# Gate projection on contiguous rows, and convolution taps kept in DRAM, in a streaming-encoder layer

## The chip, the cores and the metric

The kernel runs on all 8 cores of one Trainium2 chip. The time is the device time of the slowest core, in microseconds (us). The unchanged kernel takes about 1606 us.

Most executions of one kernel agree within 0.3%. In some executions here the cores of one die, or of both, show a lower TensorE clock and the time is some 3 to 15% longer.

## The reference

One layer: a half-step FFN, then a mixing stage with chunked attention and a depthwise convolution side by side, then another half-step FFN.

```python
D_MODEL = 1024; BATCH = 4; SEQ = 4096
D_ATTN = 512; N_HEADS = 8; D_CONV = 512; CONV_WIDTH = 31; D_FF = 2816

x = x + 0.5 * swiglu(rmsnorm(x, g1), ...)               # FFN 1
z = rmsnorm(x, mix_norm) @ w_in                         # q | k | v | a | b, 512 each
attn_out = chunk_band_attention(q, k, v, rel_bias)      # 64-frame chunks, 576-key band
g  = a * sigmoid(b)                                     # the gate product (GLU)
dw = causal depthwise conv of g, width 31, + bias
conv_out = silu(layernorm(dw))
x = x + concat(attn_out, conv_out) @ w_out
x = x + 0.5 * swiglu(rmsnorm(x, g2), ...)               # FFN 2
y = rmsnorm(x, final_norm)
```

## The kernel before

Each core computes 2048 rows, in two groups (0 and 1) of 768 and 1280 rows; activations stand transposed, with channels on the 128 partitions and rows along the free dimension. Each group passes through FFN 1, the mixing stage and FFN 2.

All instructions are placed by a list scheduler that runs when the program is built. It has a cost model: a duration for every operation and a landing time for every DMA. Each engine then executes its instructions **in that fixed order** (in the changed kernel DVE stands still for 21.02 us before a copy while an attention product waits behind it), so a wrong duration in the model does not only misjudge a time, it can also put instructions at places where they block others.

```python
def op(self, e, fn, dur, reads=(), writes=(), inc=True):
    start = max(self.t[e], ...)            # when the model thinks its inputs are there
    self.t[e] = start + dur                # dur: the model's cost figure
    E.items.append(("op", fn, inc))        # its fixed place in the engine's stream

def dma(self, e, fn, semname, nbytes, ..., late=2.0):
    beg = max(self.t[e], self.dma_free)
    self.dma_free = beg + nbytes / 300e3
    fin = max(self.dma_free, ...) + late   # when the model thinks it lands

def act(out, in_, func, n, ...):   P.op("act", ..., 0.19 + n / 1400.0, ...)
def dve(fn, n, ..., rate=960.0):   P.op("dve", fn, 0.07 + n / rate, ...)
def pool(fn, n, reads, writes):    P.op("pool", fn, 0.1 + n / 700.0, reads, writes)
```

Weights pass through a ring buffer in one fixed order, called pieces. POOL's DMA queue loads a piece as soon as the pieces that stood in its place are released. The convolution is 16 x 9 matmuls per group with "spread taps": matrices of 128 x 2304 bf16 per piece, mostly zeros. They are made in the ring, by a multiplication on POOL or DVE, each time they are needed:

```python
for c in range(4): addp((gi, "ab", c), wab_d[c], 2048)         # gate weights
for j in range(4): addp((gi, "K", j), wk_d[j], 1024)
for i in range(8):
    if i == VPOS: addp((gi, "V"), wv_d, 4096)
    addp((gi, "cv", i), i, 2304)                               # taps: made, not loaded
for j in range(4): addp((gi, "Q", j), wq_d[j], 1024)
for i in range(2): addp((gi, "wo%d" % i), wout_d[i], 4096)     # w_out, 1 MB each
for i in range(6): addp((gi, fi, "gu", i), wgu_d[fi][i], 4096) # next FFN, 1 MB each

def issue_weights():
    while ws["next"] < len(pieces):
        p = pieces[ws["next"]]
        # ... return while a piece that overlaps p is not released ...
        if isinstance(p.src, int):
            (pool, dve)[p.src % 2](lambda h: h.tensor_tensor(out=o_, in0=i0, in1=i1, op=ALU.mult),
                                   p.n, ("cmp", "cb"), (("w", p.id),))
            continue
        P.dma("pool", lambda h: h.dma_start(out=dst, in_=src), ...)
```

The gate projection wants its result in *phase order* (all rows 0, 4, 8, ..., then 1, 5, 9, ...), because the convolution works on four phases. It gets that order by streaming the input `hT` with every fourth column:

```python
def glu(g):
    ...
    for ab, b in ((1, bB), (0, bA)):
        for kc in range(8):
            rhs = hT[:, kc, c0:c0 + n].rearrange("p (u s) -> p s u", s=4)
            mm(b, 0, wv[:, ab, kc, :], rhs, n, kc == 0, kc == 7, ...)
    act(tt, bb, AF.Sigmoid, ...)
    gd = gTs[gi][:, c, :, ua:ua + n // 4]
    dve(lambda h: h.tensor_tensor(out=gd, in0=a4, in1=t4, op=ALU.mult), ...)   # a4, t4: views in phases
    # after channels 1 and 3: DMA to DRAM (gscr) and back as gp, with phases on the partitions
```

The convolution's output takes a similar way. After its layer norm it is stored to DRAM (`cscr`), read back in another layout, and copied by DVE into `cvt`, the operand of w_out. I call the load the **way back** and the copies the **cvt copies**. They run beside the attention, whose last step, the **attention product**, is on DVE too; PE may not start the next head pair's product with V before it, because it empties the PSUM banks.

```python
def conv_ln(g):
    ...
    for pc in range(2):
        for p4 in range(4):
            P.dma("sp", ... dma_start(out=cr_d..., in_=co...))                 # cscr <- dreg
    for j in range(4):
        P.dma("sp", ... dma_start(out=c2s..., in_=cr_d...), ..., late=4.0)     # dreg <- cscr, the way back
    for s in g.main:
        for c in range(4):
            yield lambda: max(P.est("dve", (("c2", gi, c),)) - 0.2, P.t["dve"] - 1.0)
            dve(lambda h: h.tensor_copy(out=o_, in_=i_), 4 * un, ...)          # cvt copy

def fin1(u):                                                                   # in attention
    ...
    for e in range(2):
        dve(lambda h: h.tensor_tensor(out=o_, in0=i0, in1=i1, op=ALU.mult), n, # attention product
            (("ps", 4 + e), ("rs", ri)), (("q", gi, j, s),))
```

The softmax here doesn't subtract the row's maximum and nothing guards it: scores larger than these inputs give would overflow.

Of the kernel before, what the change touches and what calls it, by code (L numbers as in the profile page):

```python
# [8 lines left out]
BF16 = mybir.dt.bfloat16  # L9
AF = mybir.ActivationFunctionType  # L10
ALU = mybir.AluOpType
# [34 lines left out]
B_I32 = 2560  # L46
# [198 lines left out]
def build_nc(debug=None):  # L245
# [13 lines left out]
    wv_d = din("wv", [128, 4096])  # L259
    gs_d = [nc.dram_tensor("gscr%d" % g.gi, [32, 16, 4, g.U + g.hist // 4], BF16).ap() for g in G]  # L260
# [7 lines left out]
    with ExitStack() as es:  # L268
# [43 lines left out]
        Pb = carve(O_P, 4096, BF16).rearrange("p (i e t) -> p i e t", i=2, e=2)  # L312
        tmpF = carve(O_RS, 4096, F32).rearrange("p (i t) -> p i t", i=2)
# [9 lines left out]
        stage = carve(O_ACC, CB_N * 4, F32)  # L323
        kM = at_f[:, 0:4 * TMAX].rearrange("p (j t) -> p j t", j=4)
# [44 lines left out]
        for i in range(2):  # L369
            P.reg(("P", i), "d", O_P + 2048 * i, O_P + 2048 * (i + 1))  # L370
            P.reg(("tmpF", i), "d", O_RS + 2048 * i, O_RS + 2048 * (i + 1))
            P.reg(("rs", i), "d", O_RS + 2048 * i, O_RS + 2048 * (i + 1))
# [4 lines left out]
        P.reg("gph", "d", O_GP, O_GP + 16 * 2 * GW)  # L377
        P.reg("stage", "d", O_ACC, O_ACC + CB_N * 4)
# [45 lines left out]
        def pool(fn, n, reads, writes):  # L424
            P.op("pool", fn, 0.1 + n / 700.0, reads, writes)
# [9 lines left out]
        class Piece:  # L435
            def __init__(self, src, ncols):
                self.src, self.n = src, ncols
                self.off = None
                self.issued = False
                self.released = False  # L440
# [4 lines left out]
        def addp(name, src, n):  # L445
            p = Piece(src, n)
            p.id = len(pieces)
            pieces.append(p)
            wp[name] = p
        for gi in range(2):  # L450
            for fi in range(2):
                if fi == 1:
# [4 lines left out]
                    for i in range(8):  # L457
                        if i == VPOS:
                            addp((gi, "V"), wv_d, 4096)
                        addp((gi, "cv", i), i, 2304)  # L460
# [21 lines left out]
        def issue_weights():  # L482
            while ws["next"] < len(pieces):
# [6 lines left out]
                if isinstance(p.src, int):  # L490
                    o_ = ring[:, p.off:p.off + p.n].rearrange("p (a c) -> p a c", c=32)
                    i0 = cmp_t[:, 72 * p.src:72 * (p.src + 1)].unsqueeze(2).broadcast_to([128, 72, 32])
                    i1 = cb[:, B_I32:B_I32 + 32].unsqueeze(1).broadcast_to([128, 72, 32])
                    (pool, dve)[p.src % 2](
                        lambda h, o_=o_, i0=i0, i1=i1: h.tensor_tensor(out=o_, in0=i0, in1=i1, op=ALU.mult), p.n,  # L495
                        ("cmp", "cb"), (("w", p.id),))
                    continue
                k = 2 if p.id == 0 else 1
                w = p.n // k
                for i in range(k):  # L500
# [3 lines left out]
                          "w0" if p.id == 0 else "w%d" % (1 + p.id % 16), 512 * w, reads=(), writes=(("w", p.id),),  # L504
                          issue=1.0, total=2 if p.id == 0 else None)
# [294 lines left out]
        def glu(g):  # L800
# [9 lines left out]
            if True:  # L810
                for c, (s, c0, n) in todo:
# [19 lines left out]
                    for ab, b in ((1, bB), (0, bA)):  # L831
                        for kc in range(8):
                            rhs = hT[:, kc, c0:c0 + n].rearrange("p (u s) -> p s u", s=4)
# [6 lines left out]
                    ua = (c0 - g.H + g.hist) // 4  # L840
                    gd = gTs[gi][:, c, :, ua:ua + n // 4]
                    a4 = ab_.rearrange("p (s u) -> p s u", s=4)
                    t4 = tt.rearrange("p (s u) -> p s u", s=4)
                    dve(lambda h, gd=gd, a4=a4, t4=t4: h.tensor_tensor(out=gd, in0=a4, in1=t4, op=ALU.mult), n,
                        (("ps", bA), ("rs", ti)), (("g", gi, c),))
# [355 lines left out]

        def setup_tables():
# [5 lines left out]
            for hh in range(8):  # L1208
# [14 lines left out]
                yield lambda: P.t["dve"] - 1.0  # L1223
            hv = stage[:, CB_HV:CB_HV + 64]
# [25 lines left out]
        S.add(1, setup_tables())  # L1250
        loads += [(G[1], s) for s in G[1].ids]
# [167 lines left out]
```

## Time and profile before

| Before | value |
|---|---|
| median of 6 runs | 1605.91 us (1605.15 to 1709.28; two slow runs, 1684.16 and 1709.28) |
| spans of the cores in the profiled run | 1594.9 to 1605.5 us |
| mean granted TensorE clock of the cores | 0.979 to 0.985 |

The page's first part gives each engine's busy time, share of the span and number of instructions; its fourth part follows the chain of work that ended last and gives the share of each engine in it.

```profile
PE 1503.6 (94%) x8535; PEld 815.3 (51%) x8670; DVE 545.4 (34%) x867; ACT 457.0 (28%) x762; POOL 296.8 (18%) x334
...
PE 82%; issue 4%; DVE 4%; POOL 4%; ACT 3%; DMA 2%; SPq 0%; POOLq 0%; DVEq 0%; ACTq 0%
```

TensorE (PE) bounds the kernel: it is busy for 94% of the span and is 82% of the chain.

The next lines are from the timeline of PE in the second mixing stage. The columns are start, length in us, engine, line of the program, operation, output <- inputs, sizes, and the number of instructions in the row. Line 414 is the helper that issues every matmul, so rows are told apart by their operands: `psA<-hT,ring` is here the gate, `ps<-hT,ring` the K projection.

```profile
1023.91 7.39 PE L414 MATMUL psA<-hT,ring 128*128 128x512 bf16 x16
...
1031.36 1.67 PE L414 MATMUL ps<-hT,ring 128*128 128x512 bf16 x7
```

A gate matmul of 512 columns takes about 7.39 / 16 = 0.46 us, a K matmul on contiguous columns of the same `hT` 1.67 / 7 = 0.24 us with the pipeline's tail, 0.216 us in longer rows. The stride of four bf16 doubles the cost.

The taps, in the groups of costliest instructions (busy us, mean ns of one, idle time before them and its releasers):

```profile
L495 POOL TENSOR_TENSOR ring<-cmp_sb,cb_sb 128x2304 bf16<-128x2304 bf16 x8 | 33.3, 4159 | 108.3 <-PE psA L414 93.4 <-PE ps L414 14.9
L495 DVE TENSOR_TENSOR ring<-cmp_sb,cb_sb 128x2304 bf16<-128x2304 bf16 x8 | 31.8, 3978 | 1.6 <-issue 1.6
```

What PE waited for, in us in total, number of times, longest. L1132 is the attention product, L969 the convolution's bias, L495 a tap multiplication:

```profile
PE ps L414 <- DVE dreg L1132: 10.6, 11, 1.7
PE ps L414 <- DVE dreg L969: 8.7, 3, 5.9
...
PE ps L414 <- POOL ring L495: 2.1, 1, 2.1
```

From the chain that ended last (start, length in us, what):

```profile
472.78 26.47 DMA cscr<-dreg
501.37 3.78 DMA dreg<-cscr
```

A store to `cscr` took 26.47 us, while four weight loads of 1 MB were in flight; the way back itself took 3.78 us.

### The profile page before, as it was taken

The page shows a single profiled execution, that of the slowest core. Times are in us where ns is not written, and L with a number is a line of the kernel's source. Part 1 is how long each engine was busy: PE and PEld are TensorE (multiplying, and loading weights), DVE is VectorE, ACT ScalarE, POOL GpSimd, SP SyncE. Part 2 cuts the span into 40 slices and gives each one's busy share as a digit, 9 for nine tenths or more (in the row PEclk, how much of TensorE's full clock was granted, in tenths as well). Part 3 has the DMA queues.
Part 4 walks back from the last instruction along what each step waited for, and adds up shares of the span by engine and source line. Part 5 has one row for each costly group of instructions (what it writes and reads, how often), then busy time and mean ns, then how long its engine had stood idle before and what let it go on. Part 6 is the DMA issues. An engine that isn't in the chain of part 4 may idle for free.

```text
span 1605.5 us, 23614 instructions; the slowest of 8 cores (1594.9 to 1605.5 us)
## 1 busy us (share of the span) xinstructions
PE 1503.6 (94%) x8535; PEld 815.3 (51%) x8670; DVE 545.4 (34%) x867; ACT 457.0 (28%) x762; POOL 296.8 (18%) x334
## 2 busy tenths in 40 slices
PE   8899999989878899978999999999878999999996
PEld 5455555543534566644555554434434455555553
DVE  1432221263432522227322222624633442222226
ACT  2321011232176410145110112311386741101123
POOL 2300000251610300063000002503600320000023
PEclk9999999999999999999999999999979999999998
DMA  8342423350434466522943323203242044242313
GB/s 183 92 73 40 73 50 62 60 106 11 77 62 91 100 125 118 102 43 53 227 91 57 73 50 56 40 17 60 43 85 61 1 80 72 40 73 53 60 33 132
DMA packets 29985, 117.41 MB, mean 73 GB/s; under 512 B 7088, under 2 KB 12336, under 8 KB 22064
## 3 DMA queue, kind: packets, MB, share of 16 engines
q0 software_dynamic: 15552, 84.04, 29.9%
q1 hardware_dynamic: 14320, 31.85, 6.7%
q8 instruction: 72, 1.18, 0.3%
q14 instruction: 41, 0.34, 0.1%
HBM read 187.30 MB, written 12.62 MB: 125 GB/s over the span
## 4 chain that ended last, share of the span: by engine, by line
PE 82%; issue 4%; DVE 4%; POOL 4%; ACT 3%; DMA 2%; SPq 0%; POOLq 0%; DVEq 0%; ACTq 0%
PE psA L414 52%; PE ps L414 28%; POOL ssum L568 3%; PE ps L405 2%; DVE hT L605 2%; DMA cscr<-dreg 2%; ACT dreg L418 2%; ACT L418 1%; DVE dreg L1132 1%; DVE dreg L605 0%; DVE xres L747 0%; POOL ssb L573 0%; ACT sq L418 0%; POOL dreg L983 0%; POOL ring L495 0%
## 5 line engine op out<-in xcount | busy, mean ns | idle before, releaser
L414 PE MATMUL psA<-hT,ring 128*128 128x512 bf16 (+2 forms) x4185 | 813.1, 355 | 15.7 <-DVE hT L605 11.7
L414 PEld LDWEIGHTS psA<-hT,ring 128*128 128x128 bf16 x4256 | 418.9, 100 | 404.5 <-issue 91.1
L418 ACT ACTIVATE dreg<-psA 128x512 f32<-128x512 f32 (+3 forms) x350 | 217.2, 625 | 826.1 <-PE psA L414 818.4
L414 PE MATMUL ps<-at,ring 128*128 128x512 bf16 (+1 forms) x1909 | 344.9, 341 | 2.8 <-ACT rstd L418 1.1
L717 DVE TENSOR_TENSOR at<-psA,dreg 128x512 bf16<-128x512 f32 (+1 forms) x242 | 143.9, 595 | 520.4 <-PE psA L414 499.5
L414 PEld LDWEIGHTS ps<-at,ring 128*128 128x128 bf16 x1936 | 189.4, 98 | 156.1 <-issue 3.6
L568 POOL TENSOR_TENSOR ssum<-ssum,sq 128x512 f32<-128x512 f32 (+1 forms) x132 | 137.4, 1041 | 245.1 <-ACT sq L418 233.5
L747 DVE SCALAR_TENSOR_TENSOR xres<-ps,xres 128x512 f32<-128x512 f32 (+1 forms) x176 | 103.3, 592 | 218.7 <-PE ps L414 214.5
L418 ACT ACTIVATE sq<-xres 128x512 bf16<-128x512 f32 (+1 forms) x140 | 76.5, 554 | 130.1 <-DVE xres L747 73.1
L503 POOL DMA_DIRECT2D ring<-wgu x45 | 24.3, 540 | 467.7 <-PE psA L414 231.0
L414 PE MATMUL ps<-dreg,ring 128*128 128x512 bf16 (+3 forms) x599 | 91.7, 310 | 11.9 <-DVE dreg L969 8.7
L605 DVE SCALAR_TENSOR_TENSOR hT<-xres,cs_sb,rstd 128x512 bf16<-128x512 f32 (+1 forms) x120 | 88.8, 793 | 38.7 <-ACT rstd L418 38.7
L414 PEld LDWEIGHTS ps<-dreg,ring 128*128 128x128 bf16 x608 | 57.5, 99 | 40.9 <-issue 13.6
L414 PE MATMUL ps<-hT,ring 128*128 128x512 bf16 (+1 forms) x342 | 65.7, 347 | 0.6 <-issue 0.2
L405 PE MATMUL ps<-cb_sb 128*128 128x256 bf16 x460 | 57.1, 285 | 9.3 <-POOL ssb L573 4.3
L418 ACT ACT_TABLE_LOAD x39 | 50.0, 1283 | 40.5 <-PE psA L414 15.3
L495 POOL TENSOR_TENSOR ring<-cmp_sb,cb_sb 128x2304 bf16<-128x2304 bf16 x8 | 33.3, 4159 | 108.3 <-PE psA L414 93.4
L405 PEld LDWEIGHTS ps<-cb_sb 128*128 128x128 bf16 x460 | 46.9, 102 | 12.3 <-issue 4.5
L414 PE MATMUL ps<-dreg,at 128*128 128x256 bf16 (+3 forms) x222 | 39.3, 284 | 13.7 <-ACT dreg L418 8.3
L414 PEld LDWEIGHTS ps<-hT,ring 128*128 128x128 bf16 x352 | 34.9, 100 | 30.5 <-issue 4.8
L1132 DVE TENSOR_TENSOR dreg<-ps,dreg 64x512 bf16<-64x512 f32 (+1 forms) x40 | 23.3, 582 | 71.5 <-ACT dreg L418 70.8
L503 POOL DMA_DIRECT2D ring<-wdA x16 | 8.4, 528 | 207.3 <-PE psA L414 207.3
(68 smaller groups left out, 610.9 us busy)
## 6 DMA issues: line engine op xcount, KB each, us to landing
ring<-wgu POOLq DMA_DIRECT2D x43, 1024.0 KB, 9.7
ring<-wdA POOLq DMA_DIRECT2D x16, 768.0 KB, 7.7
ring<-wdB POOLq DMA_DIRECT2D x16, 640.0 KB, 7.3
yout<-dreg SPq DMA_DIRECT2D x3, 2048.0 KB, 6.7
ring<-wab POOLq DMA_DIRECT2D x8, 512.0 KB, 8.1
xres<-xin SPq DMA_DIRECT2D x2, 2048.0 KB, 20.2
ring<-wout POOLq DMA_DIRECT2D x4, 1024.0 KB, 13.2
xres<-xin SPq DMA_DIRECT2D x6, 512.0 KB, 8.4
```

Source lines behind the costliest of these rows:

```text
L405: P.op("pe", lambda h: h.matmul(o, lhsT=onesS, rhs=cb[:, B_ONES:B_ONES + 256], start=True, stop=True, skip_group_check=True), 0.11, ("cb1" ...
L414: P.op("pe", lambda h: h.matmul(o, lhsT=lhsT, rhs=rhs, start=start, stop=stop, skip_group_check=True), max(n / 2370.0, 0.06) if dur is Non ...
L418: P.op("act", lambda h: h.activation(out=out, in_=in_, func=func, **kw), 0.19 + n / 1400.0, reads, writes)
L495: lambda h, o_=o_, i0=i0, i1=i1: h.tensor_tensor(out=o_, in0=i0, in1=i1, op=ALU.mult), p.n,
L503: P.dma("pool", lambda h, dst=dst, src=src: h.dma_start(out=dst, in_=src), "w0" if p.id == 0 else "w%d" % (1 + p.id % 16), 512 * w, reads= ...
L568: pool(lambda h: h.tensor_tensor(out=ss, in0=ss, in1=sqt, op=ALU.add), n, (("ssum", r), ("sq", i)), (("ssum", r),))
L605: dve(lambda h, dst=dst, xin=xin, gcol=gcol: h.scalar_tensor_tensor(out=dst, in0=xin, scalar=gcol, in1=rt, op0=ALU.mult, op1=ALU.mult), n, ...
L717: dve(lambda h, at=at, ub=ub, tt=tt: h.tensor_tensor(out=at, in0=ub, in1=tt, op=ALU.mult), n, (("ps", bU), ("tmpF", ti)), (("AT", gi, fl, ...
L747: dve(lambda h, xo=xo, bk=bk: h.scalar_tensor_tensor(out=xo, in0=bk, scalar=0.5, in1=xo, op0=ALU.mult, op1=ALU.add), n, (("ps", b), xk), ( ...
L1132: dve(lambda h, o_=o_, i0=i0, i1=i1: h.tensor_tensor(out=o_, in0=i0, in1=i1, op=ALU.mult), n, (("ps", 4 + e), ("rs", ri)), (("q", gi, j, s),))
```

## The change

It has two intended parts, and it also corrects one figure of the cost model.

1. **Gate part.** The gate matmuls stream contiguous columns. The product goes to a small tile `gn`; one more copy per tile, by ACT or DVE, puts it into phase order.
2. **Tap part.** The spread taps are made once, by POOL near the start, written to DRAM as bf16, and loaded through the ring like weights, 0.59 MB a piece.
3. **Figure.** The cost of a POOL operation in the model goes from 0.1 + n/700 to 0.25 + n/650 us.

```diff
+    cw_d = nc.dram_tensor("cwscr", [8, 128, 2304], BF16).ap()
+        gn = carve(O_P, 2048, BF16).rearrange("p (i t) -> p i t", i=2)
+        cwb = carve(O_GP, 9216, BF16).rearrange("p (i c) -> p i c", i=2)
...
-            P.op("pool", fn, 0.1 + n / 700.0, reads, writes)
+            P.op("pool", fn, 0.25 + n / 650.0, reads, writes)
...
-                        addp((gi, "cv", i), i, 2304)
+                        addp((gi, "cv", i), cw_d[i], 2304, (("cw", i),))      # reads: its store has landed
...
-                if isinstance(p.src, int):
-                    ...  (the multiplication on POOL or DVE)
...
-                            rhs = hT[:, kc, c0:c0 + n].rearrange("p (u s) -> p s u", s=4)
+                            rhs = hT[:, kc, c0:c0 + n]
...
+                    dve(lambda h, ...: h.tensor_tensor(out=gnt, in0=ab_, in1=tt, op=ALU.mult), n, ...)
                     gd = gTs[gi][:, c, :, ua:ua + n // 4]
-                    dve(lambda h, ...: h.tensor_tensor(out=gd, in0=a4, in1=t4, op=ALU.mult), n, ...)
+                    g4 = gnt.rearrange("p (u s) -> p s u", s=4)
+                    if P.t["act"] < P.t["dve"]:
+                        act(gd, g4, AF.Copy, n, ...)
+                    else:
+                        dve(lambda h, ...: h.tensor_copy(out=gd, in_=g4), n, ...)
...
+        def setup_conv():
+            yield lambda: P.est("pool", ("cmp", "cb"), ()) if ("tables",) in F else INF
+            for i in range(8):
+                ...
+                P.op("pool", lambda h, ...: h.tensor_tensor(out=o_, in0=i0, in1=i1, op=ALU.mult), 4.1,
+                     ("cmp", "cb"), (("cwb", i % 2),))
+                P.dma("sp", lambda h, ...: h.dma_start(out=cw_d[i], in_=w_), "cw%d" % i, 256 * 2304, ...)
...
+            F.add(("tables",))         # in setup_tables, just before its last step, 16 small casts on DVE
...
+        S.add(1.5, setup_conv())
```

More of the change, by code (lines that the diff above doesn't have):

```diff
@@ L369, in build_nc @@
         for i in range(2):
+            P.reg(("gn", i), "d", O_P + 1024 * i, O_P + 1024 * (i + 1))
             P.reg(("P", i), "d", O_P + 2048 * i, O_P + 2048 * (i + 1))
@@ L377, in build_nc @@
         P.reg("gph", "d", O_GP, O_GP + 16 * 2 * GW)
+        for i in range(2):
+            P.reg(("cwb", i), "d", O_GP + 4608 * i, O_GP + 4608 * (i + 1))
         P.reg("stage", "d", O_ACC, O_ACC + CB_N * 4)
@@ L435, in build_nc, with __init__ @@
         class Piece:
-            def __init__(self, src, ncols):
-                self.src, self.n = src, ncols
+            def __init__(self, src, ncols, reads):
+                self.src, self.n, self.reads = src, ncols, reads
                 self.off = None
@@ L443, in build_nc, with addp @@
         wp = {}
-        def addp(name, src, n):
-            p = Piece(src, n)
+        def addp(name, src, n, reads=()):
+            p = Piece(src, n, reads)
             p.id = len(pieces)
@@ L489, in issue_weights @@
                 p.issued = True
-                if isinstance(p.src, int):
-                    o_ = ring[:, p.off:p.off + p.n].rearrange("p (a c) -> p a c", c=32)
-                    i0 = cmp_t[:, 72 * p.src:72 * (p.src + 1)].unsqueeze(2).broadcast_to([128, 72, 32])
-                    i1 = cb[:, B_I32:B_I32 + 32].unsqueeze(1).broadcast_to([128, 72, 32])
-                    (pool, dve)[p.src % 2](
-                        lambda h, o_=o_, i0=i0, i1=i1: h.tensor_tensor(out=o_, in0=i0, in1=i1, op=ALU.mult), p.n,
-                        ("cmp", "cb"), (("w", p.id),))
-                    continue
                 k = 2 if p.id == 0 else 1
@@ L503, in issue_weights @@
                     P.dma("pool", lambda h, dst=dst, src=src: h.dma_start(out=dst, in_=src),
-                          "w0" if p.id == 0 else "w%d" % (1 + p.id % 16), 512 * w, reads=(), writes=(("w", p.id),),
-                          issue=1.0, total=2 if p.id == 0 else None)
+                          "w0" if p.id == 0 else "w%d" % (1 + p.id % 16), (256 if p.reads else 512) * w,
+                          reads=p.reads, writes=(("w", p.id),), issue=1.0, total=2 if p.id == 0 else None)
         def wsl(p, view):
@@ L840, in glu @@
                     ua = (c0 - g.H + g.hist) // 4
+                    gi_ = nxt("gn", 2)
+                    gnt = gn[:, gi_, 0:n]
+                    dve(lambda h, gnt=gnt, ab_=ab_, tt=tt: h.tensor_tensor(out=gnt, in0=ab_, in1=tt, op=ALU.mult), n,
+                        (("ps", bA), ("rs", ti)), (("gn", gi_),))
                     gd = gTs[gi][:, c, :, ua:ua + n // 4]
-                    a4 = ab_.rearrange("p (s u) -> p s u", s=4)
-                    t4 = tt.rearrange("p (s u) -> p s u", s=4)
-                    dve(lambda h, gd=gd, a4=a4, t4=t4: h.tensor_tensor(out=gd, in0=a4, in1=t4, op=ALU.mult), n,
-                        (("ps", bA), ("rs", ti)), (("g", gi, c),))
+                    g4 = gnt.rearrange("p (u s) -> p s u", s=4)
+                    if P.t["act"] < P.t["dve"]:
+                        act(gd, g4, AF.Copy, n, (("gn", gi_),), (("g", gi, c),))
+                    else:
+                        dve(lambda h, gd=gd, g4=g4: h.tensor_copy(out=gd, in_=g4), n, (("gn", gi_),), (("g", gi, c),))
                     left[c] -= 1
@@ L1200, in wout @@
             F.add(("wout", gi))
+        def setup_conv():
+            yield lambda: P.est("pool", ("cmp", "cb"), ()) if ("tables",) in F else INF
+            i1 = cb[:, B_I32:B_I32 + 32].unsqueeze(1).broadcast_to([128, 72, 32])
+            for i in range(8):
+                yield lambda: P.est("pool", (), (("cwb", i % 2),))
+                w_ = cwb[:, i % 2, :]
+                o_ = w_.rearrange("p (a c) -> p a c", c=32)
+                i0 = cmp_t[:, 72 * i:72 * (i + 1)].unsqueeze(2).broadcast_to([128, 72, 32])
+                P.op("pool", lambda h, o_=o_, i0=i0: h.tensor_tensor(out=o_, in0=i0, in1=i1, op=ALU.mult), 4.1,
+                     ("cmp", "cb"), (("cwb", i % 2),))
+                P.dma("sp", lambda h, w_=w_, i=i: h.dma_start(out=cw_d[i], in_=w_), "cw%d" % i, 256 * 2304,
+                      reads=(("cwb", i % 2),), writes=(("cw", i),), issue=0.6)
         def setup_tables():
```

## The prediction

> **What bounds it now.** TensorE. The page's busy table gives PE 1503.6 of 1605.5 us (94%), the chain that ended last is 82% PE, and the granted clock is 0.98. DVE (34%), ACT (28%) and POOL (18%) matter only where PE waits for them.
>
> **What the change removes.**
> 1. The gate projection (GLU) streams hT with every fourth column, to leave the result in phase order. In the chain such a matmul of 512 columns takes 452 ns (14.46 us for 32; 7.23 us for 16); the K projection, on contiguous columns of the same hT, takes 216 ns, and the FFN 217 ns. [...]this trace says a stride of four doubles the cost. GLU streams 4 x 16 x (768 + 1280) = 131,072 columns in the two groups (plus 32-column pieces). At 0.883 against 0.421 ns a column that is 60.5 us of PE: 22.7 in the first group (window 347–403 us), 37.8 in the second (1024–1100 us). PE is saturated in both windows, so nearly all of it is on the path.
> 2. Sixteen tap multiplications (L495: 8 on POOL at 4.16 us, 8 on DVE at 2.6 to 9.6 us) in the mixing stage. Off PE, but PE waits behind them: at 351 us a POOL one stretches two DVE norm ops to 4.99 us (PE idle 3.1); in the first convolution gaps of 0.56 + 2.27 + 2.10 us; in the second 5.89 us, behind a 9.6 us DVE tap. [...]Sum on the path: about 14 us.
>
> **What it adds.**
> - 20 products plus 20 strided copies: about 0.77 us on DVE (like the 128x512 copies of L1044) or 0.6 on ACT. A unit takes PE 3.45 us, so they hide, except the last before each transfer to phase order: 2 x 0.8 us.
> - Eight POOL tap multiplications, once (33 us). The tables are ready about 96 us, when POOL has finished the starting norms (last at 72 us) and is idle until about 300 us but for weight issues. Cost 0 to 2 us.
> - 16 loads of 0.59 MB as bf16 by POOL's queue. The comparable loads land in 5 to 10 us, in order with V (issued after the last K matmul). cv5 to cv7 may come a few us late; V matmuls fill. About 2 us.
> - New waits: GLU's 3.45 us units catch up with the norm of the last 256-column block, so K matmuls (17 us in all per group) are used sooner, and less remains to cover the 11 to 13 us from the last gate product to gp landing. I allow 4 us a group, 8 in all.
>
> **Sum.** 1606 - 60.5 - 14 + 1.6 + 1 + 2 + 8 = 1544; 80% range 1530 to 1558. Chances: faster 0.97, same 0.025, slower 0.005.
>
> **What would show each step.** Timeline: GLU matmuls of 512 at about 216 ns, GLU of 16 in 3.45 us; PE busy near 1445 us with the same number of matmuls. Groups: L495 gone from the mixing stages, eight POOL multiplications near 100 to 150 us, all L605 norm ops near 1 us. Waits: PE behind DVE L969 and POOL ring falls from 11 to about 2 us; new PE waits before the first convolution matmul, at most 5 us a group. FFN stages unchanged within 1 us each.
>
> **What would make it wrong.** A lower granted clock once GLU runs dense; tap loads queueing behind V so that the convolution stalls with nothing to fill; the scheduler, whose cost model changed, ordering attention worse; POOL taps at the start delaying norms or weight loads.

No term of the sum goes with them; it came to 1606 - 60.5 - 14 + 1.6 + 1 + 2 + 8 = 1544 us, and the 14 us are the waits read from the trace (3.1 + 0.56 + 2.27 + 2.10 + 5.89).

## More of the kernel before

One more view matters later: DVE's timeline in the first attention (L1132 attention product, L1044 cvt copy; in brackets the idle time before the row, and what ended it).

```profile
476.39 1.41 DVE L1132 TENSOR_TENSOR dreg<-ps,dreg 64x512 bf16<-64x512 f32 x2 [4.52 <-ACT dreg L418]
...
495.98 1.41 DVE L1132 TENSOR_TENSOR dreg<-ps,dreg 64x512 bf16<-64x512 f32 x2 [8.07 <-ACT dreg L418]
...
505.24 1.31 DVE L1044 COPY dreg<-dreg 128x512 bf16<-128x512 bf16 x2 [7.85 <-DMA dreg<-cscr]
```

The cvt copies wait 7.85 us for the way back. In this order it harms little: three attention products (one row each, for a pair of heads) stand before the copies, and PE never waits over 1.7 us for one.

## The result, and the profile after

| | before | after |
|---|---|---|
| median, us | 1606.43 (20 runs, the later ones included; at least 3 of them slow) | 1584.07 (10 runs, 2 of them slow) |
| range, us | 1605.15 to 1709.28 | 1580.11 to 1730.44 |
| ratio of fast runs, 95% interval | | 0.9858 (0.9849 to 0.9868) |
| spans of the cores, profiled run | 1594.9 to 1605.5 us | 1566.6 to 1583.1 us |
| granted clock of the cores | 0.979 to 0.985 | 0.971 to 0.978 |

A ratio here and below is the mean time of one kernel's fast runs over that of the other's in the same rounds, so it is not quite the ratio of the medians quoted. The change saves 1.4%, within the 2% that counts as the same. The prediction, 1544 us with a range of 1530 to 1558, was wrong by 40 us.

The same parts of the page after:

```profile
PE 1473.2 (93%) x8826; PEld 826.3 (52%) x8826; DVE 518.8 (33%) x860; ACT 464.3 (29%) x783; POOL 297.4 (19%) x350
...
PE 78%; DMA 5%; DVE 5%; issue 4%; ACT 3%; POOL 3%; SPq 1%; DVEq 0%; POOLq 0%; ACTq 0%
```

PE's share of the chain fell from 82% to 78%, and DMA's rose from 2% to 5%: the chain now passes through transfers. The span fell by 22 us, but PE's work fell by more than it seems. Its busy time counts filler matmuls, which the scheduler places into PE's waits and whose result nobody uses: their group rose from 460 matmuls in 57.1 us to 616 in 75.0 us. The rest of PE's work fell by 48 us.

The gate itself did what it should. PE's timeline, after:

```profile
1024.23 3.62 PE L420 MATMUL psA<-hT,ring 128*128 128x512 bf16 x16
...
1029.52 10.52 PE L420 MATMUL psA<-hT,ring 128*128 128x512 bf16 x48
```

That is 10.52 / 48 = 0.219 us a matmul, 3.62 us for sixteen instead of 7.39. The copies into phase order all went to ACT; in the groups the ones of 512 columns read:

```profile
L424 ACT ACTIVATE dreg<-dreg 128x512 bf16<-128x512 bf16 x12 | 8.0, 669 | 19.5 <-DVE dreg L841 19.5
```

What PE waits for has changed (slowest core, core 1; L1135 is the attention product, L765 a copy of a Q tile out of PSUM, L715 an FFN product):

```profile
PE ps L420 <- DVE dreg L1135: 22.8, 10, 19.1
PE ps L420 <- DVE dreg L765: 16.2, 1, 16.2
...
PE psA L420 <- DVE at L715: 5.4, 1, 5.4
```

Three single waits, of 19.1, 16.2 and 5.4 us, come to 40.7 us, about the size of what is missing; the stages below and the experiments have to say whether that is more than a coincidence. To place them, I read the first matmul of every stage from the timelines of all eight cores. The table gives the median length of each stage over the cores, in us (the some 30 us before the first FFN matmul and 11 after the last matmul are in no row).

| stage | before | after | difference |
|---|---|---|---|
| start and FFN 1, group 0 | 314.8 | 318.9 | +4.1 |
| gate and K, group 0 | 68.6 | 48.5 | -20.1 |
| convolution, group 0 | 39.8 | 38.3 | -1.5 |
| attention and w_out, group 0 | 90.8 | 105.7 | +14.9 |
| FFN 2, group 0, and start of group 1 | 201.7 | 204.4 | +2.7 |
| FFN 1, group 1 | 274.1 | 274.0 | -0.1 |
| gate and K, group 1 | 90.8 | 57.6 | -33.2 |
| convolution, group 1 | 43.2 | 40.5 | -2.7 |
| attention and w_out, group 1 | 134.2 | 138.8 | +4.6 |
| FFN 2, group 1 | 301.7 | 303.2 | +1.5 |

In the ninth row the cores differ: 132.5 to 135.5 us before, but 135.5 to 148.0 after. On the slowest cores that stage lost some 13 us or more, and it is the slowest core that sets the time. So the gate stages give 53.3 us and the convolutions 4.2; some 15 + 14 us go in the two attentions, 4 at the start, 4 elsewhere.

What happens in the first attention shows in DVE's timeline (core 1; L1135 attention product, L1047 cvt copies):

```profile
456.98 1.41 DVE L1135 TENSOR_TENSOR dreg<-ps,dreg 64x512 bf16<-64x512 f32 x2 [1.81 <-ACT dreg L424]
...
483.18 2.72 DVE L1047 COPY dreg<-dreg 128x512 bf16<-128x512 bf16 x5 [21.02 <-DMA dreg<-cscr]
485.70 1.43 DVE L1135 TENSOR_TENSOR dreg<-ps,dreg 64x512 bf16<-64x512 f32 x2
```

and in PE's:

```profile
486.54 1.31 PE L420 MATMUL ps<-dreg,vh 128*128 128x512 bf16 x2 [19.13 <-DVE dreg L1135]
```

The copies now stand after the *first* attention product rather than the third. DVE comes to them at 462 us and does nothing else until the way back lands at 483 us; the second attention product stands behind them, and PE stands behind that. DMA issues of the same stretch, with KB each and the median us from issue to landing, say why the landing is late:

```profile
ring<-wout POOLq DMA_DIRECT2D x2, 1024.0 KB, 14.1
ring<-wgu POOLq DMA_DIRECT2D x2, 1024.0 KB, 20.5
...
dreg<-cscr SPq DMA_DIRECT2D x4, 192.0 KB, 23.7
```

Four weight loads of 1 MB are issued between 452.0 and 462.2 us, around the four small ones of the way back (452.5 us). These take 23.7 us, where the model adds 4 us to the time of the bytes (`late=4.0`).

The 16.2 us wait in group 1 is of the same kind, on cores 1 and 2: PE waits there for a copy of a Q tile that stands behind the cvt copies in DVE's order. The trace also shows why the cores differ. On core 0 the last store to `cscr` is issued at 1145.97 us, before the first w_out load at 1146.66, and every store lands within 2.8 us; on core 1 the last two are issued at 1149.48 and 1150.01 us, after that load at 1149.11, and land some 17 us later, so that the way back starts at 1168.27 us instead of 1149.43; core 2 is the same. (Core 5 shows the late stores too, but with w_out at 1141.58 us, and ends between.) So less than a microsecond between two queues goes with some 10 us of this stage.

A gap also costs clock. The stretches of core 1 (us of the window, its length, busy time of PE, PEld, DVE, ACT, POOL, then the granted clock, the share of the DMA engines and GB/s):

```profile
467.00:486.00 19.00, 0.41 (x4) 0.12 (x2) 2.82 (x6) 0.91 (x1) 0.00 (x0) 0.59 0.79 153
486.00:490.00 4.00, 3.32 (x16) 1.03 (x16) 2.12 (x5) 0.97 (x1) 0.00 (x0) 0.50 0.00 0
490.00:494.00 4.00, 3.93 (x36) 2.12 (x32) 0.00 (x0) 2.51 (x4) 0.00 (x0) 0.91 0.00 0
```

After the gap PE runs at half clock for some 4 us: 0.50, against 1.00 before it (455 to 467 us); in e4_hold below, which takes the wait away, the clock is 1.00 in every stretch from 455 to 498 us (core 1). So the lower mean clock of the kernel after, 0.971 to 0.978, looks like a consequence of the waits rather than a cause of the loss; the mean clock of e4_hold, 0.980 to 0.986, agrees.

### The profile page after: what moved, and what is told of

Read it like the earlier page. It is cut to its first block, busy times and chain, and to the rows that moved or that the text cites. A ratio compares the mean times of both kernels' runs of the same rounds, so it can differ in the third digit from the quotient of the medians.

```text
span 1583.1 us, 24095 instructions; the slowest of 8 cores (1566.6 to 1583.1 us)
## 1 busy us (share of the span) xinstructions
PE 1473.2 (93%) x8826; PEld 826.3 (52%) x8826; DVE 518.8 (33%) x860; ACT 464.3 (29%) x783; POOL 297.4 (19%) x350
## 4 chain that ended last, share of the span: by engine, by line
PE 78%; DMA 5%; DVE 5%; issue 4%; ACT 3%; POOL 3%; SPq 1%; DVEq 0%; POOLq 0%; ACTq 0%
PE psA L420 49%; PE ps L420 27%; DMA dreg<-cscr 3%; PE ps L411 2%; DVE hT L603 2%; POOL ssum L566 2%; ACT dreg L424 2%; DMA cscr<-dreg 1%; DMA dreg<-gscr 1%; ACT L424 1%; DMA gscr<-dreg 1%; DVE xres L745 1%; DVE vh L1245 1%; DVE dreg L603 0%; POOL ssb L571 0%
## 5 line engine op out<-in xcount | busy, mean ns | idle before, releaser
L420 PE MATMUL psA<-hT,ring 128*128 128x512 bf16 (+2 forms) x4256 | 763.5, 341 | 19.5 <-DVE hT L603 12.9
L420 PEld LDWEIGHTS psA<-hT,ring 128*128 128x128 bf16 x4256 | 414.2, 99 | 364.4 <-issue 42.7
L715 DVE TENSOR_TENSOR at<-psA,dreg 128x512 bf16<-128x512 f32 (+1 forms) x242 | 143.8, 595 | 520.5 <-PE psA L420 496.8
L420 PE MATMUL ps<-hT,ring 128*128 128x512 bf16 (+1 forms) x352 | 66.1, 343 | 16.2 <-DVE dreg L765 16.2
L411 PE MATMUL ps<-cb_sb 128*128 128x256 bf16 x616 | 75.0, 282 | 4.3 <-DVE cb_sb L1253 4.3
L411 PEld LDWEIGHTS ps<-cb_sb 128*128 128x128 bf16 x616 | 62.3, 101 | 14.3 <-issue 4.3
L1135 DVE TENSOR_TENSOR dreg<-ps,dreg 64x512 bf16<-64x512 f32 (+1 forms) x40 | 23.3, 583 | 73.6 <-ACT dreg L424 73.0
L420 PE MATMUL ps<-dreg,vh 128*128 128x128 bf16 (+2 forms) x64 | 15.0, 313 | 29.3 <-DVE dreg L1135 21.3
```

The costliest lines, as they stand in the source:

```text
L411: P.op("pe", lambda h: h.matmul(o, lhsT=onesS, rhs=cb[:, B_ONES:B_ONES + 256], start=True, stop=True, skip_group_check=True), 0.11, ("cb1" ...
L420: P.op("pe", lambda h: h.matmul(o, lhsT=lhsT, rhs=rhs, start=start, stop=stop, skip_group_check=True), max(n / 2370.0, 0.06) if dur is Non ...
L715: dve(lambda h, at=at, ub=ub, tt=tt: h.tensor_tensor(out=at, in0=ub, in1=tt, op=ALU.mult), n, (("ps", bU), ("tmpF", ti)), (("AT", gi, fl, ...
L1135: dve(lambda h, o_=o_, i0=i0, i1=i1: h.tensor_tensor(out=o_, in0=i0, in1=i1, op=ALU.mult), n, (("ps", 4 + e), ("rs", ri)), (("q", gi, j, s),))
```

## The experiments

**Theory A (collision and order).** Both parts save what they should, but the new fixed order puts the cvt copies in front of the attention products while the way back is under way beside four weight loads. A smaller loss is at the start, where the taps on POOL hold up the last casts of the tables on DVE.

**Rival R (the tap part itself).** Sixteen more loads of 0.59 MB disturb everything else, so the tap part costs more than it saves wherever it is used, and the gate part alone would reach about 1550 us.

**Rival, the figure.** The corrected POOL figure alone reorders the program for the worse.

Experiments e1, e2, e4 and e5 were timed on one chip, e3, e8_all, e8v and e9 on a second, e0, e10 and e11 on a third, each beside the kernel before (fast median 1606 to 1608 us).

### e1_glu: the gate part alone

The kernel before with the gate part and the new POOL figure; taps as before.

```diff
-                            rhs = hT[:, kc, c0:c0 + n].rearrange("p (u s) -> p s u", s=4)
+                            rhs = hT[:, kc, c0:c0 + n]
+                    (gn, the product and the copy as in the change; 0.25 + n / 650.0)
```

> Only the gate part of the change (contiguous rows, product, copy; the POOL cost figure of the changed kernel kept); the taps are made in place in the mixing stages as before. Theory A (the gate saves what was forecast, and the gain is then given back in attention, where VectorE waits in order for the way back from channel order, plus small losses at the start and at the tap loads): stage from first GLU to first convolution matmul about 49 and 58 to 60 us as in the changed kernel, first FFN back to 274 us, attention of the first group still lengthened by 5 to 15 us; time 1565 to 1585 us. Rival R (the taps' way through DRAM eats the gain): time near 1550 us and no lengthened attention.

Measured: 1564.33 us (1562.1 to 1564.4), ratio 0.9732 (0.9715 to 0.9748), correct. Gate stages 51.2 and 60.0 us instead of 68.6 and 90.8; first attention 94.8.

The gate part alone is worth 42 us, and 20 us *more* than the whole change. The time lies just under the range of theory A and well over what R wanted, so both missed, A by less than a microsecond. A's mechanism did not show here either: the first attention is 4.0 us longer than before, but that comes with the POOL figure alone (94.8 us in e0_figure below), and the copies stand behind five attention products. What follows for certain is only that the tap part, as it stands in this order, costs some 20 us.

### e2_taps: the tap part alone

The changed kernel with the strided gate put back.

```diff
-                            rhs = hT[:, kc, c0:c0 + n]
+                            rhs = hT[:, kc, c0:c0 + n].rearrange("p (u s) -> p s u", s=4)
+                    (the product straight into phase order, as before)
```

> Only the tap part (made once on POOL, written to DRAM, 16 loads); the gate matmuls stride as before. Theory A: 1596 to 1612 us: the first FFN 5 to 8 us longer, each convolution waits about 5 us for its last taps, the old tap waits gone. Rival R: 1630 us or more, with the loss in the mixing stages.

Measured: fast runs 1635.38 to 1642.12 us (one slow run, 1805), ratio 1.0198 (1.0173 to 1.0222), correct. First attention 105.8 us, second 135.4 to 146.8 over the cores, start 321.3.

Theory A's forecast for this run missed: I had thought the order went wrong only with both parts together. R had the size. But the loss stands in the same places as in the full change: a PE gap of 19.1 us behind the attention product, 15.6 behind a Q copy, 5.3 at the start. So the tap part brings the bad order. Whether the extra loads also cost something where they stand needs the next runs.

### e4_hold: w_out loads held until the way back has landed

The transfers no longer collide. The two w_out pieces, and with them all that follow in the ring, are issued only after the way back. The order of instructions on PE, ACT, DVE and SP stays exactly as in the changed kernel, and POOL's too.

```diff
-                        addp((gi, "wo%d" % i), wout_d[i], 4096)
+                        addp((gi, "wo%d" % i), wout_d[i], 4096, tuple(("c2", gi, c) for c in range(4)))
 ...
+                if p.reads and p.reads[0][0] == "c2" and ("c2", p.reads[0][1]) not in F:
+                    return
 ...    (after the way back is issued, in conv_ln)
+            F.add(("c2", gi))
+            issue_weights()
```

> The changed kernel, with the loads of w_out (and so the weights queued behind them) held until the way back from channel order has landed; the order of instructions on PE, ACT and DVE is the same. Theory A: the four loads of the way back land in under 8 us instead of 21 to 24; PE's gap of 18 to 19 us behind the attention product in the first group shrinks to under 3 us, the 5 to 16 us gap behind the q copy in the second too; attention plus w_out of the first group back to about 91 us from 106; time 1550 to 1566 us. Rival S (attention is bound by ScalarE or by its own chain, and the gap only moves): time within 8 us of 1584.

Measured: 1548.70 us (1548.3 to 1550.1), ratio 0.964 (0.9626 to 0.9655), correct; a little faster than the expected range. First attention 86.0 us instead of 105.7; second 130.6 to 130.7 on all cores instead of 135.5 to 148.0.

DMA issues of the same stretch, DVE's timeline and PE's waits (core 6; L1051 cvt copies, L1139 attention product):

```profile
ring<-wgu POOLq DMA_DIRECT2D x2, 1024.0 KB, 24.4
...
dreg<-cscr SPq DMA_DIRECT2D x4, 192.0 KB, 3.7
```

```profile
463.31 2.74 DVE L1051 COPY dreg<-dreg 128x512 bf16<-128x512 bf16 x5
...
468.20 1.41 DVE L1139 TENSOR_TENSOR dreg<-ps,dreg 64x512 bf16<-64x512 f32 x2 [2.15 <-ACT dreg L424]
```

```profile
PE ps L420 <- DVE dreg L1139: 5.3, 13, 0.7
```

The way back lands in 3.7 us instead of 23.7, and the copies, at the same place in DVE's order, wait for nothing. PE's longest wait behind the attention product falls from 19.1 to 0.7 us. That is theory A's main point, and it is worth 35 us. So here transfers of SP's queue are slowed by loads of POOL's: four loads of 192 KB take six times as long beside four of 1 MB.

Rival R falls as far as the attention goes: all sixteen tap loads are still there.

### e5_tab: taps after the whole table stage

The first tap multiplication waits also for the 16 small casts on DVE that end the table stage. In POOL's order two weight issues move with it; the other engines keep theirs.

```diff
-            yield lambda: P.est("pool", ("cmp", "cb"), ()) if ("tables",) in F else INF
+            yield lambda: P.est("pool", ("cmp", "cb", ("vh", 3)), ()) if ("tables",) in F else INF
 ...
-                     ("cmp", "cb"), (("cwb", i % 2),))
+                     ("cmp", "cb", ("vh", 3)), (("cwb", i % 2),))
```

> The changed kernel, with the first tap multiplication waiting for the 16 small casts of the table stage; nothing else moved but the place of two weight issues in POOL's queue. Theory A[...]: the 16 casts take about 1.7 us again instead of 8.7, PE's 5.3 us gap behind the FFN product disappears, first FFN 275 to 276 us instead of 281; time 1575 to 1581 us. If the loss is only put off, the first FFN stays at 281 us.

Measured: fast runs 1575.89 to 1577.74 us (one slow run, 1750), ratio 0.9814 (0.9798 to 0.983), correct. Start and FFN 1: 310.3 us instead of 318.9.

Timelines of the start, first of the changed kernel (core 1): POOL makes two taps (L1213), DVE does the casts (L1245), PE waits for an FFN product that stands behind them.

```profile
92.74 8.04 POOL L1213 TENSOR_TENSOR dreg<-cmp_sb,cb_sb 128x2304 bf16<-128x2304 bf16 x2 [23.21 <-DVE cb_sb L1236]
...
93.53 8.73 DVE L1245 CAST vh<-dreg 128x64 bf16<-128x64 f32 x16
...
102.74 9.44 PE L420 MATMUL psA<-hT,ring 128*128 128x256 bf16 x34 [5.36 <-DVE at L715]
```

Then of e5_tab (core 4):

```profile
90.84 1.71 DVE L1245 CAST vh<-dreg 128x64 bf16<-128x64 f32 x16
...
93.21 8.06 POOL L1213 TENSOR_TENSOR dreg<-cmp_sb,cb_sb 128x2304 bf16<-128x2304 bf16 x2
```

The casts take 1.71 us when POOL is idle and 8.73 us beside two taps, and the start loses 7 to 9 us by it. In the changed kernel the first two casts take 3.30 and 4.08 us, each until a tap ends, and the other fourteen 0.18 us each (0.25 for one) after the second tap. By what means a tap holds a cast is not shown; not every operation on DVE is held, for a product out of PSUM takes its usual 0.69 us beside a later tap (at 110.19 us, core 1). The prediction had read such a stretch from the trace, two norm operations at 4.99 us, for what the change *removes*; I had not looked for it in what the change adds.

### e3_late: the model is told the truth about the landing

No transfer is moved. Only the model's landing time of the way back is changed, so that the scheduler places the copies later.

```diff
-                      issue=0.6, total=4, late=4.0)
+                      issue=0.6, total=4, late=26.0)
```

> The changed kernel; only the landing time that the scheduler assumes for the way back is 26 us instead of 4, so that the copies into cvt stand later in VectorE's queue; no transfer is moved. If the loss needs both the slow landing and VectorE's order, this recovers much of what holding the weights recovered: PE's gap behind the attention product in the first group falls from 18 to 19 us to under 5 us although the way back still lands after 20 us or more; time 1550 to 1568 us. If the slow transfers themselves are what costs (w_out waits for cvt whatever the order), 1575 to 1590 us, with the gap moved to before w_out.

Measured: fast runs 1558.21 and 1556.62 us; the other two were slow (1726, 1793), so there is no ratio with an interval. The kernel before gave 1605.9 to 1610.8 us in its fast runs. Correct. First attention 87.3 us, second 129.6.

DMA issues, DVE's timeline and PE's waits (core 6):

```profile
dreg<-cscr SPq DMA_DIRECT2D x4, 192.0 KB, 23.0
```

```profile
486.76 1.41 DVE L1135 TENSOR_TENSOR dreg<-ps,dreg 64x512 bf16<-64x512 f32 x2 [7.62 <-ACT dreg L424]
488.20 1.89 DVE L1047 COPY dreg<-dreg 128x512 bf16<-128x512 bf16 x3
```

```profile
PE ps L420 <- DVE dreg L1135: 8.5, 10, 1.2
```

The way back is as slow as in the changed kernel, 23.0 us, but the copies come after the landing and the long gap is gone. So neither the slow landing nor the early place does the harm alone: it takes both, and mending either mends it. Most of the gap to e4_hold, some 9 us, lies in the start (320.6 us against 318.0) and in the start of group 1 (209.1 against 204.2); why was not tested.

### e8_all: both mends together

The edits of e4_hold and e5_tab.

```diff
+                        addp((gi, "wo%d" % i), wout_d[i], 4096, tuple(("c2", gi, c) for c in range(4)))   # and the rest of e4_hold
+            yield lambda: P.est("pool", ("cmp", "cb", ("vh", 3)), ()) if ("tables",) in F else INF         # and the rest of e5_tab
```

> The changed kernel with both repairs (w_out loads held until the way back has landed, first tap after the small casts). The two losses lie in different stages, so they should add: 1548.7 - 7 = 1541 to 1543 us; first FFN 272 to 273 us, attention of the first group 50 us. If POOL's start-up order mattered only through the slowest core, 1546 us or more.

Measured: 1543.28 us (1542.8 to 1544.8), ratio 0.9601 (0.9585 to 0.9617), correct. This is the fastest version; it beats the kernel before by 4.0% and the change as it was given by some 41 us. Its stages: start 310.2, gate 48.6, convolution 38.3, attention 86.0, FFN 204.5, FFN 1 274.0, gate 57.8, convolution 40.0, attention 130.6, FFN 304.5. The savings add up: e4's 35 and e5's 7 make 42, and 41 were measured (on different chips, each beside the kernel before).

### e9_gluhold: is the tap part any good, once mended?

The kernel of e1_glu (taps made in the ring, as before) with the hold of e4_hold.

```diff
+                        addp((gi, "wo%d" % i), wout_d[i], 4096, tuple(("c2", gi, c) for c in range(4)))
+                if p.reads and ("c2", p.reads[0][1]) not in F:
+                    return
+            F.add(("c2", gi))
+            issue_weights()
```

> The gate part alone (taps in place, as before) with the w_out loads held until the way back has landed. Shows what the taps' way through DRAM is worth once the attention wait is mended in both: attention plus w_out of the first group from 95 to 86 to 90 us; time 1548 to 1558 us. Theory A: 5 to 12 us slower than e8_all (in-place taps still make the convolutions wait, 40.4 and 42.2 against 38.3 and 40.5). Rival R (the DRAM way is a loss in itself): faster than e8_all.

Measured: 1563.56 us (1563.1 to 1564.2), ratio 0.9726 (0.971 to 0.9741), correct. That is no better than e1_glu, and a miss: I expected 1548 to 1558, and 5 to 12 us more than e8_all, not 20.

In e1_glu the way back landed in 3.6 us already, as its DMA issues show; what met the loads there were the stores. DMA issues of e1_glu, then of e9_gluhold (both core 1):

```profile
cscr<-dreg SPq DMA_DIRECT2D x8, 96.0 KB, 18.0
```

```profile
cscr<-dreg SPq DMA_DIRECT2D x8, 96.0 KB, 2.0
```

The hold mended them, from 18.0 to 2.0 us, but nobody had waited: the copies stood behind five attention products. (With the hold the scheduler put them behind the second, so the order changed too.) I should have read that before the run. What the run does show is the worth of the tap part where neither version waits for the copies: e8_all is 20 us faster than e9_gluhold. By stages the gate gains 2.8 + 2.6 us, the convolution 2.1 + 2.6, the attention 7.7 + 3.7. So rival R, as it was put, falls: the tap part is a saving, and the first order hid it. In the gate and the convolution, where the taps themselves stood, it is 10 us, near the net that I had put down; the 11 in the attention come with another order of instructions, and how much of them the taps cause is not shown.

Of the 7.7 us in the first attention, 5.9 are PE's waits for ACT, 10.9 us in e9_gluhold and 5.0 in e8_all (core 1). ACT's timeline of e9_gluhold at that point shows whom PE waits behind:

```profile
438.07 2.75 ACT L420 ACTIVATE dreg<-dreg,cs_sb 128x192 bf16<-128x192 f32 x6
440.84 1.28 ACT L420 ACT_TABLE_LOAD   x1
442.13 1.94 ACT L420 ACTIVATE dreg<-psA 128x1024 bf16<-128x1024 f32 x2
```

The attention's exponentials (`dreg<-psA`) alternate there with the convolution's swish (`128x192`), with a table load of 1.28 us at each turn; in e8_all 14 of the swish's 16 instructions are done before the first exponential. Why the scheduler arrives at that was not tested.

### e8v: V behind the taps in the ring

In the changed kernel the convolution waits for its sixth tap piece, whose load stands behind V's 1 MB (5.51 us of filler matmuls stand before that piece's matmuls, core 1). This version is e8_all with V moved behind the last tap piece.

```diff
-                        if i == VPOS:
-                            addp((gi, "V"), wv_d, 4096)
                         addp((gi, "cv", i), cw_d[i], 2304, (("cw", i),))
+                    addp((gi, "V"), wv_d, 4096)
```

> As e8_all, with the V weights after the last tap piece in the ring instead of before cv5, so that cv5 to cv7 do not queue behind V. If the 5 us of filler matmuls in each convolution come from that queue: convolution stages 33 and 35 us instead of 38.3 and 40.5, unless V then arrives late and V's matmuls wait instead; time 1530 to 1538 us if V is in time, 1538 to 1545 us if the wait only moves to V.

Measured: fast runs 1553.25 to 1554.79 us (one slow run, 1734), ratio 0.9666 (0.9648 to 0.9684), correct. A miss, 11 us slower than e8_all.

The convolution stages became longer, 43.1 and 45.3 us instead of 38.3 and 40.0, and the first attention shorter, 81.8 instead of 86.0, but the second longer, 134.0 instead of 130.6. The V matmuls had filled the time of the convolution's waits; with V late, they no longer can. The wait was moved, not removed.

### e0_figure: the POOL figure alone

```diff
-            P.op("pool", fn, 0.1 + n / 700.0, reads, writes)
+            P.op("pool", fn, 0.25 + n / 650.0, reads, writes)
```

> The kernel before with only the assumed cost of a POOL operation changed (0.25 us + n/650 instead of 0.1 + n/700), which the changed kernel carries too. It moves the cvt copies behind more attention products in VectorE's order. If the figure is part of what lost the gain, slower than before by 5 us or more; if it is a help or nothing (the copies stand later, so the slow way back should do less harm), 1595 to 1607 us.

Measured: fast runs 1609.02 and 1609.64 us; two runs were slow (1680, 1770), so there is no interval. The kernel before gave 1605.0 to 1609.5 us in its fast runs of the same rounds. Correct. Both expectations missed, each by 2 to 3 us. Stages: start 310.4 us (-4.4), first attention 94.8 (+4.0), start of group 1 207.4 (+5.7).

The figure alone shifts some microseconds between stages and changes the total by about +2 us, too little to call. With it as a base, the gate part is worth about -45 us (e1_glu against e0_figure), and the tap part about +30 (e2_taps against e0_figure).

### e11_oldfig: the mended version with the old figure

e8_all, with

```diff
-            P.op("pool", fn, 0.25 + n / 650.0, reads, writes)
+            P.op("pool", fn, 0.1 + n / 700.0, reads, writes)
```

> e8_all with the old assumed POOL cost. The figure only orders; with the way back landing early the order should matter little: 1538 to 1552 us. If it is below 1541 it is the best version.

Measured: 1545.25 us (1544.9 to 1546.8), ratio 0.9618 (0.9603 to 0.9634), correct. Two microseconds from e8_all. The rival of the figure falls: it is not what decides. DVE's timeline of this run also bears on where the early place comes from: with the tap part and the old figure, two of the cvt copies (441.50 us, core 1) stand before even the first attention product (443.40 us). This run has the hold too, which left the place alone in e4_hold but moved it in e9_gluhold; a rebuild of the changed kernel with the old figure and no hold, not run on the chip, gives the same place.

### e10_stride2 and e10_stride8: what a stride costs

The kernel before with the gate's step changed from four elements (8 bytes) to two (4 bytes) or eight (16 bytes). The columns then come in a wrong order, so the result is wrong; matmuls and sizes are the same.

```diff
-                            rhs = hT[:, kc, c0:c0 + n].rearrange("p (u s) -> p s u", s=4)
+                            rhs = hT[:, kc, c0:c0 + n].rearrange("p (u s) -> p s u", s=2)   # or s=8
```

> The kernel before, wrong result on purpose: the gate matmuls take every second column (4 bytes apart) instead of every fourth (8 bytes). If the cost of a strided read grows with the step, a 512-column gate matmul takes about 216 to 330 ns against 452 ns at step four; if any step halves the rate, 452 ns.

> The kernel before, wrong result on purpose: the gate matmuls take every eighth column (16 bytes apart). If the cost grows with the step, 700 to 900 ns for 512 columns; [...]if any step merely halves the rate, 452 ns.

Measured, one run each: 1558.14 us with step 2 and 1727.5 with step 8, beside 1605.0 to 1609.5 of the kernel before. PE's timelines, step 2 (core 2):

```profile
1020.55 7.36 PE L414 MATMUL psA<-hT,ring 128*128 128x512 bf16 x32
1027.74 1.89 PE L414 MATMUL ps<-hT,ring 128*128 128x512 bf16 x8
```

and step 8 (core 7), with the matmuls of K that follow the gate:

```profile
1068.48 14.56 PE L414 MATMUL psA<-hT,ring 128*128 128x512 bf16 x16
1082.86 3.59 PE L414 MATMUL ps<-hT,ring 128*128 128x512 bf16 x8
1086.25 14.58 PE L414 MATMUL psA<-hT,ring 128*128 128x512 bf16 x16
```

Counted from the start of one row to the start of the next, which leaves the pipeline's tail out, a gate matmul of 512 columns takes 216 ns on contiguous columns, 225 with a step of 4 bytes, 452 with 8 and 899 with 16. Here the step of 4 bytes is nearly free, and each of the two further doublings doubles the time.

With step 8 the granted clock falls to half in the gate (0.50), and the K matmuls there take (1086.25 - 1082.86) / 8 = 424 ns instead of 216. So I checked whether the 899 ns are the stride's or the clock's. Two stretches of 4 us in the gate, with the columns as above (length; busy time of PE, PEld, DVE, ACT, POOL; clock; DMA share; GB/s):

```profile
1070.00:1074.00 4.00, 4.00 (x6) 0.59 (x5) 4.00 (x5) 0.75 (x2) 3.49 (x3) 1.00 1.05 144
1078.00:1082.00 4.00, 4.00 (x6) 0.55 (x5) 0.00 (x0) 0.00 (x0) 0.00 (x0) 0.50 0.00 0
```

Six gate matmuls touch a stretch of 4 us at either clock, and in the row of sixteen the starts are 0.90 us apart throughout, so the stride's rate does not depend on the clock here. Why the clock falls to 0.50 while the profile shows PE busy for 4.00 of 4 us was not tested; in the kernel before, with a step of 8 bytes, it stayed at 1.00 in the second gate (1030 to 1090 us). These two runs agree with the gate's term of the prediction: the time went with the stride. The step of 2 in the old order even brings 48 us by itself.

## Why the prediction was wrong

The prediction was 1544 us (1530 to 1558), with a chance of 0.97 for more than 2%. It came to 1584.07 us.

| the prediction's step | put at | the runs showed |
|---|---|---|
| gate matmuls at half the time | -60.5 us | right in the time of one: 0.219 us |
| copies into phase order | +1.6 | all went to ACT, 0.67 us each |
| new waits after the gate | +8 | with the two rows above and the 3.1 us of taps in this stage, -54.0 was forecast for the gate stages; measured -53.3 |
| waits behind taps in the convolutions | -10.8 | with the row below, -8.8 was forecast for the convolutions; measured -1.5 and -2.7 |
| tap loads behind V | +2 | too small: filler of some 5 us a group stands before the sixth tap piece |
| taps on POOL at the start | +1 ("0 to 2 us") | +4.1, although the new figure alone made the start 4.4 shorter; mending it alone was worth 7 us |
| order and transfers in attention | nothing in the sum | +14.9 in group 0, some +14 on the slowest cores in group 1 |

1. **The gate was right in its sum.** Its stages were forecast at -54.0 us and came to -53.3, and the time of one matmul was right; how the 8 us of new waits and the 1.6 of copies fell out singly was not measured, so there may be some luck in so close a sum. In group 1 PE runs the gate at a clock of 1.00 (1030 to 1050 us), so the fear of a lower clock in a dense gate did not come true there; in group 0 one stretch showed 0.55 (371 to 374 us, core 1), after one with PE busy for 1.89 of 3 us.

2. **The step that failed is one that the sum leaves out: it has no term for attention.** By leaving it out the prediction took the order on DVE and the landing of the transfers as unmoved. The runs showed +14.9 us in the first attention and some 13 or more on the slowest cores in the second, with PE waiting 19.1 us behind one attention product and 16.2 behind a Q copy. The prediction named "the scheduler, whose cost model changed, ordering attention worse" as a thing that would make it wrong, and gave it no microseconds. It happened, but not through the cost model's figure: with that alone (e0_figure) the copies stand later still, behind five attention products, and with the tap part, the hold and the old figure (e11_oldfig) they stand early all the same. It comes with the tap part, as e2_taps shows. The copies of the convolution's output moved from behind the third attention product to behind the first.

3. **The cause is a collision that was there before.** In the kernel before, four weight loads of 1 MB already met the `cscr` transfers: a store took 26.47 us, and DVE waited 7.85 us for the way back. It cost PE almost nothing, because the copies stood late. The new order put the copies early and the load took 23.7 us. e4_hold took away the collision alone (-35 us), e3_late the early place alone (about -27 us); either frees the attention.

4. **"POOL taps at the start: 0 to 2 us" was mis-sized.** I looked at whether POOL was idle, and it was. What was not idle was DVE: its 16 casts took 8.73 us instead of 1.71, two of them held until a tap ended (3.30 and 4.08 us), and PE waited 5.4 us for the product behind them.

5. **The tap part is a saving, once mended.** I had put down a net of 11 us (-14 + 1 + 2). e8_all against e9_gluhold gives 10 in the gate and the convolution, and 20 in all; the rest lies in the attention, with another order of instructions, and is not shown to be the taps' own.

6. **e8_all at 1543.3 us is not a late proof of 1544.** Its sum is made up otherwise: the first attention is 5 us shorter than before, the second 4 and the start 5, none of which I had forecast, the convolutions gain less, and the two FFN 2 rows lose 6 us. That it comes so near to 1544 is luck.

What stays open: by what steps the tap part leads the scheduler to an earlier place for the copies (the placement was read from the traces, the scheduler's choices were not taken apart), and why the swish and the exponentials alternate more in e9_gluhold.

## What to carry to other kernels

In a program with fixed instruction order, removing time in one stage can move work in another; before counting a saving, look in the trace for waits that are harmless only because of where they stand, and ask what happens if their instruction comes earlier. Here one such wait (7.85 us before, 21.02 after) took half of the gain, and holding back weight loads that nobody needed yet brought it back.

If an operation is moved to an idle engine, check also what the others do at that moment (here two taps on POOL held two casts on DVE for 3.30 and 4.08 us); and if a small transfer is on the way to the critical engine, keep large loads that are not urgent out of its few microseconds (here the small one took 3.7 us without them and 23.7 beside them).
